# Weight blocks' low parts and sums by DMAs that add onto a negated copy; gated linear attention by chunks, each head over its own 64 rows

## Chip, cores and metric

One core of one Trainium2 chip. The metric is the device time of one execution, in microseconds; less is better. Before the change it is 478.68 us, the median of 3 runs (477.87 to 479.24).

## What is computed

One decoder layer over 1088 tokens (1024 of a prompt, and 64 that are 8 sequences of 8 new tokens), model width 1024, everything in float32. With `h = RMSNorm(x)` and one projection of `h`:

```
a, gl, zc, q, k, v, zg, lr = split(h @ w_in)          # 512,512,512,256,256,512,512,16 columns
u  = a * sigmoid(gl)
cv = swish(group_layer_norm(depthwise_causal_conv(u, width 31)))
cv = (cv @ w_pw + b_pw) * silu(zc)
gk = log_sigmoid(lr @ w_alpha + b_alpha) / 16          # forget gate
o, S = gla(q, k, v, gk, S0)                            # 4 heads, keys of 64, values of 128
o  = rms_norm_per_head(o) * silu(zg)
y  = final_rms_norm(x + concat[cv, o] @ w_out)
```

`gla` is linear attention by chunks of tokens: within a chunk `o = (mask(q_t k_t^T)) v + q_t S`, and between chunks `S = S * decay + k_dec^T v`. Besides `y` the last rows of `u` and the states `S` are returned.

## The kernel before

**Split operands.** A float32 product is made of three products in the faster float32r format: an operand is split into a high part (a copy rounded to float32r) and a low part (operand minus high part), and TensorE adds high by high, high by low and low by high in PSUM. `split` (L418) does it: ScalarE copies, VectorE subtracts. `load_split` (L515) loads a weight block of 128 x 512 values into a staging buffer (`wst`, 4 slots) and splits it into the pools `wh` and `wl` (8 slots each). A weight tile of 1024 x 128 is two such halves.

**Stages.** Tokens lie along the free axis in three chunks of 384, 384 and 320 (`CHUNKS`). In order of time: loading and RMSNorm; the projections `gl` and `a` (4 tiles each); `v` of the first two heads with the low-rank gate input; `q` and `k` of these heads with the linear attention between them; `v`, then `q` and `k` of the other two heads; `zc`; `zg` with the pointwise product; and the out projection. The convolution is 31 multiply-adds of 128 x 1024 values on VectorE for each of four channel tiles; `conv_tick` gives them a low priority, so that they fill what VectorE has free up to their normalization in the `zc` and `zg` stages.

**Linear attention.** `gla_tile(p, tk)` (L765) handles one pair of heads `p` and 128 tokens. The two heads lie in the 128 rows, 64 each. `q_chunk` keeps two copies of q, each with the other head's 64 rows set to zero (by GpSimd memsets), so that a product over all 128 rows yields one head alone. A tile has a transpose of k, two products `pa` (k by q), a masked copy on VectorE, two products `pS` into 64 rows each (in the tile `px`), two of the old state by q and two of values by masked scores (both into `po`), and the update of the state. All of them are float32, which TensorE runs as two passes each; the trace counts passes.

**Out projection.** Blocks of 512 x 512 are multiplied by a scheme of seven products of sums and differences (`pr1` to `pr7`). Sums of blocks of `w_out` are made in place on VectorE (`t1` to `t4`, L1198 to L1226) out of loaded blocks, and each operand is split as above (`parts`).

**Order.** Nothing is issued as written. Each helper adds an operation with a cost to a list, and `Program.schedule` plays the list on a model of the engines: an engine takes the ready operation of the highest priority (mostly the order of writing) whose buffers are free. The instruction streams of the engines are fixed in that order, and each then runs in order on the chip. Loads and stores are issued by SyncE; GpSimd does memsets alone.

Of the kernel before, what the change touches and what calls it, by code (L numbers as in the profile page):

```python
# [14 lines left out]
P = 128  # L15
# [116 lines left out]
class Program:  # L132
# [159 lines left out]
    def issue(self, preload, after):  # L292
        order = self.schedule()
        table = next(o.table for o in order if o.table is not None)
        preload(table)
        for o in order:
            if o.table is not None and o.table != table:
                table = o.table
                preload(table)
            i = o.fn().ins  # L300
            o.name = i.name
            for tl in o.allocs:
                if tl.before is not None:
                    for name in tl.before.seen.values():
                        after(i, name)
            for tl in o.tiles:
                tl.seen[(o.eng, i.name if o.eng == "SP" else "")] = i.name
# [3 lines left out]
def build(tc, A, O):  # L311
# [68 lines left out]
    def mm(ps, lhsT, rhs, start, stop, after=None):  # L380
# [3 lines left out]
        o = prog.add("PE", lambda: T.matmul(R(ps), R(lhsT), R(rhs), start=start, stop=stop, skip_group_check=True),  # L384
                     [ps], [lhsT, rhs], c, lag=lag)
        if after is not None:
            o.deps.add(after)
        return o
# [7 lines left out]
    with ctx:  # L396
# [31 lines left out]
        mask_p = cst[:, K_MP:K_MP + 2 * P].bitcast(U32)  # L428
# [9 lines left out]
        at_p = [VT(fixed, f"at{i}", [P, 2 * P], F32, f"at{i}") for i in range(2)]  # L438
# [89 lines left out]
        def wtile(kind, i):  # L528
            return [whalf(kind, i, h) for h in range(2)]
# [107 lines left out]
        def v_weights(p):  # L637
            cols = 272 if p == 0 else 256
            return cols, [load_split(f"v{p}{i}", A[f"wv{p}"][i], 2, cols) for i in range(4)]
# [102 lines left out]
        qx = {}  # L742
        o_t = [None] * 4

        def q_chunk(p, w, c):

            ep = gx[(p, c)][0]
            n = CHUNKS[c][1]
            other = un(f"qx{p}_{c}")
            ps = proj_chunk(f"q{p}", w, c)  # L750
            lo, hi = slice(0, 64), slice(64, P)
            prog.hold = True
            zero(other[lo, :n])
            stt(other[hi, :n], ps[hi], 0.125, ep[hi, :n], ALU.mult, ALU.mult)
            stt(ep[lo, :n], ps[lo], 0.125, ep[lo, :n], ALU.mult, ALU.mult)
            zero(ep[hi, :n])
            qx[(p, c)] = ep, other
# [7 lines left out]
        def gla_tile(p, tk):  # L765
            c = tk // 3
            off = tk * P - CHUNKS[c][0]
            s = slice(off, off + P)
            q, km = qx[(p, c)], gx[(p, c)][1][:, s]
            v = vslice(p, tk)  # L770
            if tk == 0:
                for j in range(2):
                    o_t[2 * p + j] = bt(f"o{2 * p + j}")
            hs = [slice(P * j, P * j + P) for j in range(2)]
            px = pt(f"px{p}_{tk}")
            pk, pS = px[:, 0:P], px[:, P:2 * P]
            transpose(pk, km, ident)
            kT = VT(sm, "kT", [P, P], F32, f"kT{p}_{tk}")
            act(kT, pk, AF.Copy)
            pa = pt(f"pa{p}_{tk}")  # L780
            for j in range(2):
                mm(pa[:, hs[j]], km, q[j][:, s], True, True)
            at = at_p[tk % 2]
            select(at, mask_p, pa[:, 0:2 * P])
            for j in range(2):
                r = slice(64 * j, 64 * j + 64)
                mm(pS[r], kT[:, r], v[:, hs[j]], True, True)

            po = pt(f"po{p}_{tk}")
            first = None  # L790
            if tk > 0:
                for j in range(2):
                    first = mm(po[:, hs[j]], St[p], q[j][:, s], first is None, False, first)
            for j in range(2):
                first = mm(po[:, hs[j]], v[:, hs[j]], at[:, hs[j]], first is None, True, first)
            Sn = VT(sm, "S", [P, P], F32, f"S{p}_{tk}")
            cf = g_c[p][:, tk + 1:tk + 2]
            if tk == 0:
                ts(Sn, pS, cf, None, ALU.mult, None)
            else:  # L800
                Sc = VT(sm, "S", [P, P], F32, f"Sc{p}_{tk}")
                act(Sc, St[p], AF.Copy, scale=cf)
                stt(Sn, pS, cf, Sc, ALU.mult, ALU.add)
            St[p] = Sn
            for j in range(2):
                act(o_t[2 * p + j][:, tk * P:(tk + 1) * P], po[:, hs[j]], AF.Copy)
            if tk == 7:
                dma(O["gla_p"][:, p], Sn)
# [7 lines left out]
        def gla_sample(p):  # L816
            s = slice(256, 320)
            q, km = qx[(p, 2)], gx[(p, 2)][1][:, s]
            v = v_s
            prog.step, prog.shift = STEP, 0  # L820
# [7 lines left out]
            for j in range(2):  # L828
                mm(pa[0:64, hs[j]], km, q[j][:, s], True, True)
            at = at_s  # L830
            select(at[0:64], mask_s, pa[0:64, 0:P])
            q2 = un(f"q2{p}")[:, 0:P]
            for j in range(2):
                act(q2[:, hs[j]], q[j][:, s], AF.Copy)
# [3 lines left out]
            for j in range(2):  # L838
                first = mm(po[:, hs[j]], v[:, j * P:(j + 1) * P], at[:, hs[j]], j == 0, False, first)
            for b in range(NB):  # L840
                bs = slice(b * LB, (b + 1) * LB)
                mm(po.split(64)[:, :, bs], S0[:, b, :], q2[:, :, bs], False, True, first)
# [154 lines left out]
        for p in range(2):  # L997
            wq, wk = wtile("q", p), wtile("k", p)
            s0_load(p)
            for c in range(3):  # L1000
                if (p, c) not in gx:
                    gates(p, c)
                q_chunk(p, wq, c)
                conv_tick(2)
                if c > 0:
                    gla_tile(p, 3 * c - 3)
                k_chunk(p, wk, c)
                conv_tick(2)
                if c > 0:
                    gla_tile(p, 3 * c - 2)  # L1010
                    gla_tile(p, 3 * c - 1)
            if p == 0:
                wv = v_weights(1)
                for tk in range(NTT):
                    v_tile(1, wv, tk)
                    conv_tick(2)
                    if tk < 2:
                        gla_tile(0, 6 + tk)
# [8 lines left out]
            else:  # L1027
                for i in range(4):
                    w = wtile("zc", i)
                    for c in range(3):  # L1030
                        zc_chunk(i, w, c)
                        conv_tick(5)
                        if i == 0:
                            if c < 2:
                                gla_tile(1, 6 + c)
# [39 lines left out]
        for i in range(4):  # L1075
            w = wtile("zg", i)
            if i == CN_LAST:
# [4 lines left out]
                wpw += [load_split(f"pw{j}", A["w_pw"][j], 4, P) for j in range(4)]  # L1082
# [12 lines left out]
        def b_load(name, e0, h, i):  # L1095
            st = VT(wst, "wst", [P, 512], F32, f"s_{name}{i}")
            dma(st, A["w_out"][e0 + i][:, 512 * h:512 * h + 512])
            return st

        def B11(n_, i):  # L1100
            return b_load(f"b11{n_}", 0, 0, i)

        def B12(n_, i):
            return b_load(f"b12{n_}", 0, 1, i)

        def B21(n_, i):
            return b_load(f"b21{n_}", 4, 0, i)

        def B22(n_, i):
            return b_load(f"b22{n_}", 4, 1, i)  # L1110
# [9 lines left out]
        def prep(name, a, b):  # L1120
            av, bv = [], []
            for i in range(4):
                av.append(parts(f"{name}a", i, a(i)))
                bv.append(parts(f"{name}b", i, b(i)))
# [11 lines left out]
        pr1 = prep("p1", lambda i: A11[i], lambda i: B11("p", i))  # L1136
# [70 lines left out]
        def t2(i):  # L1207
            tt(T_[i], B22("t", i), T_[i], ALU.subtract)
            return T_[i]
# [9 lines left out]
        def t3(i):  # L1219
            b = B22("u", i)  # L1220
            tt(b, b, B12("u", i), ALU.subtract)
            return b

        def t4(i):
            tt(T_[i], B21("u", i), T_[i], ALU.subtract)
            return T_[i]  # L1226
# [7 lines left out]
        pr2 = prep("p2", lambda i: A12[i], lambda i: B21("p", i))  # L1234
# [14 lines left out]
        pr3 = prep("p3", s4, lambda i: B22("p", i))  # L1249
# [11 lines left out]
        b12 = [parts("b12", i, B12("p", i)) for i in range(4)]  # L1261
# [110 lines left out]
```

## Time and profile before

| | us |
|---|---|
| median of 3 runs | 478.68 |
| the profiled execution | 479.08 |
| its span, from first to last instruction | 477.0 |
| TensorE busy | 465.4 |
| VectorE busy | 416.2 |
| ScalarE busy | 297.8 |
| GpSimd busy | 9.3 |

The profile is one execution. "PE" is TensorE's matmuls, "PEld" its weight loads, DVE VectorE, ACT ScalarE, POOL GpSimd, SP SyncE. Busy time of PE contains what its pipeline overlaps, so a pace is read from the starts of neighbours, not from the duration of one. Names as `px<-v,kT` are output and inputs by the program's tile names.

### The profile page before, as it was taken

How to read it: one execution, taken by the hardware profiler on the slowest of the kernel's cores; microseconds unless marked ns; L12 is line 12 of the kernel's file. 1: busy time of each engine (PE TensorE's matmuls, PEld its weight loads, DVE VectorE, ACT ScalarE, POOL GpSimd, SP SyncE). 2: the span in 40 equal slices, each digit the busy share in tenths (PEclk: the TensorE clock that was granted, in tenths of full speed). 3: DMA queues.
4: the chain of work that ended last, by engine and by line, in shares of the span. 5: the costliest groups of instructions: out<-in, count | busy, mean ns of one | idle time of the engine just before them, and what ended most of it. 6: DMA issues, size and time to landing. Idle time of an engine off the chain costs nothing.

```text
span 477.0 us, 7890 instructions
## 1 busy us (share of the span) xinstructions
PE 465.4 (98%) x2867; PEld 436.9 (92%) x2867; DVE 416.2 (87%) x669; ACT 297.8 (62%) x794; POOL 9.3 (2%) x33
## 2 busy tenths in 40 slices
PE   7999999999999999999999999999999999999983
PEld 6899999999999999999899999999999988788763
DVE  4999999999999999999998999983527579999896
ACT  6969569816660645694643696669637465666854
POOL 1000000000000000000000000000000000000000
PEclk9999999999999999999999999999999999999998
DMA  8910391212030110030010002010101364246765
GB/s 258 357 35 1 122 180 45 57 56 56 1 123 11 40 51 7 32 123 25 28 62 21 31 1 88 23 44 24 46 33 51 119 232 152 89 142 205 239 201 218
DMA packets 33238, 43.28 MB, mean 91 GB/s; under 512 B 11696, under 2 KB 16560, under 8 KB 33200
## 3 DMA queue, kind: packets, MB, share of 16 engines
q1 hardware_dynamic: 33200, 42.78, 27.9%
q8 instruction: 22, 0.36, 0.3%
q14 instruction: 16, 0.13, 0.1%
HBM read 36.58 MB, written 6.19 MB: 90 GB/s over the span
## 4 chain that ended last, share of the span: by engine, by line
PE 88%; DVE 4%; ACT 3%; DMA 2%; issue 1%; SPq 1%; DVEq 0%
PE pv L384 11%; PE p_zc L384 10%; PE p_zg L384 10%; PE ya L384 9%; PE p_gl L384 8%; PE p_a L384 8%; PE p_k L384 5%; PE p_q L384 5%; PE pw L384 5%; PE yc L384 4%; PE po L384 3%; PE pa L384 2%; DVE xr L343 1%; PE px L384 1%; DMA s_gl<-in_w_in 1%
## 5 line engine op out<-in xcount | busy, mean ns | idle before, releaser
L339 DVE SCALAR_TENSOR_TENSOR cv<-u,par,cv 128x1024 f32<-128x1024 f32 x120 | 150.5, 1274 | 0.2
L384 PE MATMUL pv<-h_v,hh 128*128 128x272 f32 (+1 forms) x128 | 37.2, 291 | 0.0
L384 PE MATMUL pv<-l_v,hh 128*128 128x272 f32 (+1 forms) x128 | 37.0, 289 | 0.0
L384 PE MATMUL pv<-h_v,hl 128*128 128x272 f32 (+1 forms) x128 | 37.0, 289 | 0.0
L384 PE MATMUL p_gl<-hh,h_gl 128*128 128x384 f32 (+1 forms) x96 | 32.4, 338 | 1.3 <-ACT hh L333 0.8
L333 ACT ACTIVATE pr<-us,par 128x64 f32<-128x64 f32 x124 | 32.2, 346 | 0.4 <-DMA us<-in_cc 0.4
L384 PE MATMUL p_zc<-hh,h_zc 128*128 128x384 f32 (+1 forms) x96 | 32.1, 335 | 0.0
L384 PE MATMUL p_zc<-hh,l_zc 128*128 128x384 f32 (+1 forms) x96 | 31.9, 332 | 0.0
L384 PE MATMUL p_zc<-hl,h_zc 128*128 128x384 f32 (+1 forms) x96 | 31.8, 331 | 0.0
L384 PE MATMUL p_gl<-hl,h_gl 128*128 128x384 f32 (+1 forms) x96 | 31.7, 330 | 0.1
L384 PE MATMUL p_gl<-hh,l_gl 128*128 128x384 f32 (+1 forms) x96 | 31.6, 329 | 0.2 <-DVE l_gl L343 0.2
L384 PE MATMUL p_a<-hh,l_a 128*128 128x384 f32 (+1 forms) x96 | 31.7, 331 | 0.0
L384 PE MATMUL p_zg<-hh,l_zg 128*128 128x384 f32 (+1 forms) x96 | 31.4, 328 | 0.0
L384 PE MATMUL p_a<-hh,h_a 128*128 128x384 f32 (+1 forms) x96 | 31.4, 327 | 0.0
L384 PE MATMUL p_a<-hl,h_a 128*128 128x384 f32 (+1 forms) x96 | 31.4, 327 | 0.0
L384 PE MATMUL p_zg<-hl,h_zg 128*128 128x384 f32 (+1 forms) x96 | 31.4, 327 | 0.0
L384 PE MATMUL p_zg<-hh,h_zg 128*128 128x384 f32 (+1 forms) x96 | 31.4, 327 | 0.0
L384 PEld LDWEIGHTS pv<-h_v,hh 128*128 128x128 f32 x128 | 24.1, 189 | 0.4 <-issue 0.3
L384 PEld LDWEIGHTS pv<-l_v,hh 128*128 128x128 f32 x128 | 24.1, 189 | 0.3 <-issue 0.3
L384 PEld LDWEIGHTS pv<-h_v,hl 128*128 128x128 f32 x128 | 24.1, 188 | 0.0
L384 PEld LDWEIGHTS p_gl<-hh,h_gl 128*128 128x128 f32 x96 | 18.0, 188 | 2.4 <-ACT hh L333 1.4
L384 PEld LDWEIGHTS p_gl<-hl,h_gl 128*128 128x128 f32 x96 | 18.0, 188 | 0.9 <-DVE hl L343 0.4
(341 smaller groups left out, 1344.6 us busy)
## 6 DMA issues: line engine op xcount, KB each, us to landing
xr<-in_x SPq DMA_DIRECT2D x16, 256.0 KB, 3.4
out_y<-xr SPq DMA_DIRECT2D x16, 256.0 KB, 2.5
x<-in_xT SPq DMA_DIRECT2D x16, 192.0 KB, 4.7
s_gl<-in_w_in SPq DMA_DIRECT2D x8, 256.0 KB, 4.7
s_a<-in_w_in SPq DMA_DIRECT2D x8, 256.0 KB, 4.2
s_zc<-in_w_in SPq DMA_DIRECT2D x8, 256.0 KB, 2.5
s_zg<-in_w_in SPq DMA_DIRECT2D x8, 256.0 KB, 2.6
x<-in_xT SPq DMA_DIRECT2D x8, 160.0 KB, 5.2
```

Source lines behind the costliest of these rows:

```text
L333: return S.activation(R(out), R(in_), func, **kw)
L339: prog.add("DVE", lambda: V.scalar_tensor_tensor(R(out), R(a), R(s), R(b), op0, op1), [out], [a, s, b], out.n / 0.96 + 67 + 62 * isinstanc ...
L343: prog.add("DVE", lambda: V.tensor_tensor(R(out), R(a), R(b), op), [out], [a, b], out.n / 0.96 + 67)
L384: o = prog.add("PE", lambda: T.matmul(R(ps), R(lhsT), R(rhs), start=start, stop=stop, skip_group_check=True), [ps], [lhsT, rhs], c, lag=lag)
```

## The change

It has two halves. First, for the weight blocks that are loaded after the first four tiles, the low part is no longer subtracted on VectorE: ScalarE writes the negated high part into the low part's buffer, and a DMA issued by GpSimd reads the block once more from memory and adds it onto that buffer (`low_part`, `load_parts`, `b_parts`). The sums of `w_out` blocks are made in the same way (`flip`). Second, the linear attention runs by chunks of three (or two) tiles in two functions, `gla_states` and `gla_out`. The products of k by q and of state by q run over the 64 rows of their own head, so q needs no zeros and no second copy; products that lie in different halves of the array are written one after another, and the planner books each of a pair at half the cost (`pair=True`).

```diff
+    def dma_add(out, in_):
+        prog.add("POOL", lambda: G.dma_start(R(out), R(in_), accum_op=ALU.add), [out], [in_], 1100,
+                 nbytes=out.n * 4 * P, lag=2400)
...
+        def low_part(hi, lo, src):
+            act(lo, hi.bitcast(F32), AF.Copy, scale=-1.0)
+            dma_add(lo, src)
+
+        def load_parts(name, src, k, m):
+            st = VT(wst, "wst", [P, k, m], F32, f"s_{name}")
+            hi = VT(wh, "wh", [P, k, m], F32R, f"h_{name}")
+            lo = VT(wl, "wl", [P, k, m], F32R, f"l_{name}")
+            dma(st, src)
+            act(hi, st, AF.Copy)
+            low_part(hi, lo, src)
+            return hi, lo
...
         def wtile(kind, i):
-            return [whalf(kind, i, h) for h in range(2)]
+            return [load_parts(f"{kind}{i}_{h}", A["w_in"][mt[(kind, i)]][:, 4 * h:4 * h + 4, :], 4, P)
+                    for h in range(2)]
...
         def q_chunk(p, w, c):
             ep = gx[(p, c)][0]
             n = CHUNKS[c][1]
-            other = un(f"qx{p}_{c}")
             ps = proj_chunk(f"q{p}", w, c)
-            ...
+            stt(ep[:, :n], ps, 0.125, ep[:, :n], ALU.mult, ALU.mult)
...
+        def gla_states(p, c):
+            nt = 3 if c < 2 else 2
+            m = nt * P
+            km = gx[(p, c)][1]
+            pk = pt(f"pk{p}_{c}")
+            for i in range(nt):
+                transpose(pk[:, P * i:P * i + P], km[:, P * i:P * i + P], ident)
+            kT = un(f"kT{p}_{c}")
+            act(kT[:, :m], pk[:, :m], AF.Copy)
+            pS = pt(f"px{p}_{c}")
+            for i in range(nt):
+                v = vslice(p, 3 * c + i)
+                for j in range(2):
+                    mm(pS[HR[j], P * i:P * i + P], kT[:, P * i + 64 * j:P * i + 64 * j + 64], v[:, P * j:P * j + P],
+                       True, True, pair=True)
+            gs[(p, c)] = before = []
+            for i in range(nt):
+                ...
+                    act(Sc, pS[:, P * i:P * i + P], AF.Copy, scale=cf)
+                    stt(Sn, St[p], cf, Sc, ALU.mult, ALU.add)
+                St[p] = Sn
...
+        def gla_out(p, c):
+            ...
+            pa = [pt(f"pa{p}_{c}_{j}") for j in range(2)]
+            po = [pt(f"po{p}_{c}_{j}") for j in range(2)]
+            last = gs[(p, c)][-1]
+            wait = [x[2] for x in last.tile.acc if x[1]]
+            for i in range(nt):
+                s = slice(P * i, P * i + P)
+                for j in range(2):
+                    mm(pa[j][:, s], km[HR[j], s], q[HR[j], s], True, True, wait, True)
+            first = [None] * 2
+            for i in range(nt):
+                s = slice(P * i, P * i + P)
+                S_ = gs[(p, c)][i]
+                if S_ is not None:
+                    for j in range(2):
+                        first[j] = mm(po[j][:, s], S_[HR[j]], q[HR[j], s], first[j] is None, False, [first[j]], True)
+            for j in range(2):
+                select(at_p[j][:, :m].split(P), mask_p.bcast([P, nt, P]), pa[j][:, :m].split(P))
+            for j in range(2):
+                for i in range(nt):
+                    s = slice(P * i, P * i + P)
+                    first[j] = mm(po[j][:, s], vslice(p, 3 * c + i)[:, P * j:P * j + P], at_p[j][:, s], False, True,
+                                  [first[j]])
+            for j in range(2):
+                if c == 0:
                     o_t[2 * p + j] = bt(f"o{2 * p + j}")
+                act(o_t[2 * p + j][:, t0:t0 + m], po[j][:, :m], AF.Copy)
...
+        def b_parts(name, i, e0, h):
+            st, src = VT(wst, "wst", [P, 512], F32, f"s_{name}{i}"), w_blk(e0 + i, h)
+            dma(st, src)
+            t_ = VT(big, "big", [P, 2, 512], F32R, f"{name}{i}")
+            act(t_[:, 0, :], st, AF.Copy)
+            low_part(t_[:, 0, :], t_[:, 1, :], src)
+            return t_
...
+        def flip(t_, src):
+            act(t_, t_, AF.Copy, scale=-1.0)
+            dma_add(t_, src)
+            return t_
+
         def t1(i):
             T_[i] = temp("T", i)
-            tt(T_[i], B12("t", i), B11("t", i), ALU.subtract)
-            return T_[i]
+            dma(T_[i], w_blk(i, 0))
+            return flip(T_[i], w_blk(i, 1))
...
         def t2(i):
-            tt(T_[i], B22("t", i), T_[i], ALU.subtract)
-            return T_[i]
+            return flip(T_[i], w_blk(4 + i, 1))
```

`t3` and `t4` change as `t1` and `t2` do, and `b_parts` stands for `parts` on the four plain blocks of `w_out` (`pr1`, `pr2`, `pr3` and `b12`). In `gla_sample`, which handles the 64 new tokens, the zeros move into a small tile of 128 columns.

## Rows read from the trace of the kernel before

**Rows 1.** Head of the page: span, and busy time (share) and instructions of each engine.

```profile
span 477.0 us, 7890 instructions
PE 465.4 (98%) x2867; PEld 436.9 (92%) x2867; DVE 416.2 (87%) x669; ACT 297.8 (62%) x794; POOL 9.3 (2%) x33
```

**Rows 2.** Windows: busy us (instructions) of each engine in three stretches.

```profile
core 0: us, PE busy (x) PEld busy (x) DVE busy (x) ACT busy (x) POOL busy (x), PEclk, DMA share, GB/s
0.00:307.50 307.50, 304.81 (x2022) 293.51 (x2023) 288.27 (x431) 193.10 (x573) 8.06 (x30) 1.00 0.24 70
28.20:429.00 400.80, 400.80 (x2534) 382.91 (x2535) 353.71 (x536) 243.59 (x666) 7.06 (x19) 1.00 0.21 63
381.20:456.20 75.00, 73.43 (x321) 58.81 (x320) 69.53 (x123) 50.51 (x111) 0.82 (x2) 1.00 0.53 182
```

**Rows 3.** Timeline of TensorE, end of the out projection: start, us, [idle before <- releaser].

```profile
443.42 11.19 PE L384 MATMUL ya<-p7b,p7a 128*128 128x512 f32 x48
456.17 2.10 PE L384 MATMUL ya<-p4b,p4a 128*128 128x512 f32 x8 [1.57 <-DVE xr L343]
```

**Rows 4.** Groups of TensorE by form, linear attention: busy us, mean ns of a pass.

```profile
L384 PE MATMUL pa<-ge,g 128*128 128x128 f32 x32 | 6.4, 281 | 0.0
L384 PE MATMUL po<-ge,S 128*128 128x128 f32 x28 | 5.6, 282 | 0.0
```

**Rows 5.** Timeline of TensorE around one tile of the linear attention.

```profile
148.83 0.39 PE L384 MATMUL pa<-ge,g 128*128 128x128 f32 x2
149.06 0.39 PE L384 MATMUL pa<-qx,g 128*128 128x128 f32 x2
149.20 0.42 PE L384 MATMUL p_k<-hh,h_k 128*128 128x384 f32 x1
149.46 0.34 PE L384 MATMUL p_k<-hl,h_k 128*128 128x384 f32 x1
149.73 0.44 PE L384 MATMUL px<-v,kT 128*64 128x128 f32 x4
150.10 0.44 PE L384 MATMUL p_k<-hh,l_k 128*128 128x384 f32 x1
150.38 0.34 PE L384 MATMUL p_k<-hh,h_k 128*128 128x384 f32 x1
150.56 0.34 PE L384 MATMUL p_k<-hl,h_k 128*128 128x384 f32 x1
```

**Rows 6.** Timeline of TensorE, last stretch: state products of the new tokens.

```profile
467.40 2.23 PE L384 MATMUL pSs<-vs,km 64*64 64x128 f32 x32
```

**Rows 7.** Groups of VectorE and ScalarE by form: busy us, mean ns of one.

```profile
L339 DVE SCALAR_TENSOR_TENSOR cv<-u,par,cv 128x1024 f32<-128x1024 f32 x120 | 150.5, 1274 | 0.2
L349 DVE TENSOR_SCALAR cv<-u,par 128x1024 f32<-128x1024 f32 x4 | 3.2, 804 | 0.0
L343 DVE TENSOR_TENSOR l_zg<-s_zg,h_zg 128x512 fp32r<-128x512 f32 x8 | 5.5, 687 | 7.1 <-ACT h_zg L333 7.1
L333 ACT ACTIVATE h_zg<-s_zg 128x512 fp32r<-128x512 f32 x8 | 5.1, 635 | 3.4 <-PE p_zg L384 1.8 <-PE p_zc L384 1.6
```

**Rows 8.** Chain that ended last: first use of gl's third tile; a store's issue.

```profile
60.65 11.90 PE p_gl L384 x72
...
442.10 0.35 SPq L377
```

**Rows 9.** Timeline of VectorE: low parts of that tile's two halves.

```profile
50.86 1.28 DVE L343 TENSOR_TENSOR l_gl<-s_gl,h_gl 128x512 fp32r<-128x512 f32 x2
```

**Rows 10.** DMA issues: count, KB each, median us from issue to landing.

```profile
s_zg<-in_w_in SPq DMA_DIRECT2D x8, 256.0 KB, 2.6
...
fg<-in_fg SPq DMA_DIRECT2D x1, 512.0 KB, 6.8
```

**Rows 11.** Instructions on tile p1b: count, duration ns min/median/max, first and last start.

```profile
L384 PE MATMUL ya<-p1b,p1a x48: 387/390/398, 381.0 to 391.8; 128*128 128x512 f32 x48
...
L343 DVE TENSOR_TENSOR p1b<-s_b11p,p1b x4: 680/681/691, 365.5 to 380.0; 128x512 fp32r<-128x512 f32 x4
```

More of the change, by code (lines that the diff above doesn't have):

```diff
@@ L378, in dma, with mm @@
                  nbytes=v.n * 4 * (v.part[1] - v.part[0]))
-    def mm(ps, lhsT, rhs, start, stop, after=None):
+    def dma_add(out, in_):
+        prog.add("POOL", lambda: G.dma_start(R(out), R(in_), accum_op=ALU.add), [out], [in_], 1100,
+                 nbytes=out.n * 4 * P, lag=2400)
+    def mm(ps, lhsT, rhs, start, stop, after=(), pair=False):
         n, m = rhs.n, lhsT.n
@@ L384, in mm @@
         o = prog.add("PE", lambda: T.matmul(R(ps), R(lhsT), R(rhs), start=start, stop=stop, skip_group_check=True),
-                     [ps], [lhsT, rhs], c, lag=lag)
-        if after is not None:
-            o.deps.add(after)
+                     [ps], [lhsT, rhs], c / 2 if pair else c, lag=lag)
+        o.deps.update(a for a in after if a is not None)
         return o
@@ L427, in build @@
         Jr, blkr, one_r = [VT(fixed, nm, [P, P], F32R, nm) for nm in ("Jr", "blkr", "one_r")]
-        mask_p = cst[:, K_MP:K_MP + 2 * P].bitcast(U32)
+        mask_p = cst[:, K_MP:K_MP + P].bitcast(U32).split(P)
         mask_s = cst[0:64, K_MS:K_MS + P].bitcast(U32)
@@ L437, in build @@
         eps = pc(C_EPS)
-        at_p = [VT(fixed, f"at{i}", [P, 2 * P], F32, f"at{i}") for i in range(2)]
+        at_p = [VT(fixed, f"at{i}", [P, 3 * P], F32, f"at{i}") for i in range(2)]
         at_s = VT(fixed, "ats", [P, P], F32, "ats")
@@ L638, in v_weights @@
             cols = 272 if p == 0 else 256
-            return cols, [load_split(f"v{p}{i}", A[f"wv{p}"][i], 2, cols) for i in range(4)]
+            return cols, [load_parts(f"v{p}{i}", A[f"wv{p}"][i], 2, cols) for i in range(4)]
         def v_tile(p, w, tk):
@@ L763, in k_chunk @@
             tt(em[:, :n], ps, em[:, :n], ALU.mult)
[L765 to L771, printed above, removed]
-                for j in range(2):
-                    o_t[2 * p + j] = bt(f"o{2 * p + j}")
[L774 to L808, printed above, removed]
@@ L817, in gla_sample @@
             s = slice(256, 320)
-            q, km = qx[(p, 2)], gx[(p, 2)][1][:, s]
+            q, km = [t_[:, s] for t_ in gx[(p, 2)]]
             v = v_s
+            q2 = un(f"q2{p}")[:, 0:P]
+            prog.hold = True
+            zero(q2)
+            for j in range(2):
+                act(q2[HR[j], 64 * j:64 * j + 64], q[HR[j]], AF.Copy)
             prog.step, prog.shift = STEP, 0
@@ L828, in gla_sample @@
             for j in range(2):
-                mm(pa[0:64, hs[j]], km, q[j][:, s], True, True)
+                mm(pa[0:64, hs[j]], km, q2[:, hs[j]], True, True)
             at = at_s
             select(at[0:64], mask_s, pa[0:64, 0:P])
-            q2 = un(f"q2{p}")[:, 0:P]
-            for j in range(2):
-                act(q2[:, hs[j]], q[j][:, s], AF.Copy)
             q2 = q2.split(64)
@@ L838, in gla_sample @@
             for j in range(2):
-                first = mm(po[:, hs[j]], v[:, j * P:(j + 1) * P], at[:, hs[j]], j == 0, False, first)
+                first = mm(po[:, hs[j]], v[:, j * P:(j + 1) * P], at[:, hs[j]], j == 0, False, [first])
             for b in range(NB):
                 bs = slice(b * LB, (b + 1) * LB)
-                mm(po.split(64)[:, :, bs], S0[:, b, :], q2[:, :, bs], False, True, first)
+                mm(po.split(64)[:, :, bs], S0[:, b, :], q2[:, :, bs], False, True, [first])
             for j in range(2):
@@ L1081, in build @@
                     act(zc[j], zc[j], AF.Silu)
-                wpw += [load_split(f"pw{j}", A["w_pw"][j], 4, P) for j in range(4)]
+                wpw += [load_parts(f"pw{j}", A["w_pw"][j], 4, P) for j in range(4)]
             for c in range(3):
@@ L1123, in prep @@
                 av.append(parts(f"{name}a", i, a(i)))
-                bv.append(parts(f"{name}b", i, b(i)))
+                bv.append(b_parts(f"{name}b", i, *b) if isinstance(b, tuple) else parts(f"{name}b", i, b(i)))
             return av, bv
@@ L1134, in product @@
                     mm(acc[t], av[k][:, 1, ts_], bv[k][:, 0, :], False, k == 3)
-        pr1 = prep("p1", lambda i: A11[i], lambda i: B11("p", i))
+        pr1 = prep("p1", lambda i: A11[i], (0, 0))
         fg = VT(big, "big", [P, DM], F32, "fg")
@@ L1260, in build @@
         psr = pt("pys1")
-        b12 = [parts("b12", i, B12("p", i)) for i in range(4)]
+        b12 = [b_parts("b12", i, 0, 1) for i in range(4)]
         samples_half(1, True, False, pr3[1], 4, psr)
```

66 lines of the change are left out of this document (32 added, 34 removed).

## Prediction, made before the changed kernel was run

> **What bounds the kernel now.** I read the page's head first, then the windows, the waits of TensorE in its timeline, and last the linear attention in the timeline, row by row. TensorE is busy 465.4 of 477.0 us, VectorE 416.2, ScalarE 297.8 [rows 1]. From 28.2 to 429 us TensorE has no idle time at all: 400.8 of 400.8 [rows 2]. The 11.6 us that it lacks lie at the start (loads and RMSNorm), in the tail after the last product, and in one wait of 1.57 us before the last product `p4` of the out projection, which VectorE ends [rows 3]. So the time is TensorE's list of work; an edit counts where it shortens that list or where it makes TensorE wait. VectorE is the second bound: up to 307.5 us it is busy 288.3 [rows 2], much of it with the convolution's taps [rows 7].
>
> **The linear attention.** The passes of one product start some 0.11 us apart: of two neighbouring products `pa`, two passes each, the first starts at 148.83 and the second at 149.06, 0.23 us later [rows 5]. The old kernel issues 16 tiles x 2 `pa` and 14 tiles x 2 products of state by q (both kinds also on the twin copy of q): twice the 32 and 28 passes of the rows, 120 passes [rows 4], x 0.112 (0.23 / 2, less rounding) = 13.4 us.
>
> Written per head over 64 rows, two neighbours use different halves of the array. The trace has no such pair. Its nearest row is `pSs`, whose neighbours write different 64 columns of the array: 32 passes, the last starting (2.23 - 0.27 for its own length) = 1.96 us after the first, 0.063 a pass [rows 6]. Bounds: 0.112 if row halves don't overlap, 0.056 if they overlap fully. I take 0.063, by the row that is nearest: 120 x 0.063 = 7.6.
>
> Entering and leaving such a form costs something. Products of `q` or `k` at 384 columns start 0.18 apart (150.38 to 150.56); into the four passes of `px` it is 0.27 (149.46 to 149.73), out of them 0.28 (150.10 to 150.38) [rows 5]: 0.09 + 0.10 = 0.19 for an excursion. The new kernel makes the `pa` and the state products in one burst for each chunk, 6 bursts: 1.1 us. Saved: 13.4 - 7.6 - 1.1 = 4.7 us (full overlap 5.6; no overlap a loss of 1.1).
>
> The Trainium skill, TensorEngine Tiling (Array Packing), Key Properties, says that a change of tiling mode drains the engine. That speaks against the change, which puts more products into such a mode; the 0.19 us an excursion agrees with it. Its figure of up to 2x for a contraction of 64 rows would give 6.7 us for the 120 passes.
>
> The state products `pS` now make 16 excursions of four passes: 0.37 (149.73 to 150.10) + 0.19 = 0.56 each [rows 5], 9.0 us. Afterwards the same 64 passes stand in 6 groups: 64 x 0.063 + 6 x 0.19 = 5.2. Saved 3.8. Transposes and the products with values stay as many; but any float32 group between projections lengthens the next start (0.26 at 149.20 against 0.18, so 0.08 [rows 5]). At most 16 x 3 such insertions become 6 x 4, so 0 to 1.9 us; I take 0.8, since many groups stand side by side already. Together the list shortens by 4.7 + 3.8 + 0.8 = 9.3 us.
>
> Cost on the same path: a chunk now runs transposes, copy, `pS`, three state updates in a row, then `pa`, two selects of up to 384 columns, and `po`, and TensorE needs projections to fill the gaps. All of `k`, the next `q`, `v` or `zc` lies there as cover. A chunk also holds up to 6 of 8 PSUM banks. Bounds: nothing if cover suffices; 4 us a chunk, 24 us, if TensorE sat through the whole chain (a copy and three updates of some 0.8 with their handovers, two selects). I take 1 us in all, near the lower end, because the old tiles have the same kind of chain and show no idle time in the rows [rows 2].
>
> **VectorE.** A low part is 0.687 us [rows 7]. 44 go from the projections and pointwise weights, 16 from `w_out`, and 16 subtractions for sums: 76 x 0.69 = 52 us of 416. Nearly all before 307.5 us is hidden, since TensorE never waits there [rows 2]; but it is needed. If TensorE's list there gets 9.3 us shorter, VectorE would have 307.5 - 288.3 - 9.3 = 10 us of room; about 40 of the low parts lie there and give back 27. So VectorE isn't what is late next. In the out projection it is busy 69.5 of 75.0 [rows 2] and loses 28 operations, 19 us. The wait of 1.57 us before `p4` [rows 3] I count as gone: the sums for it no longer need VectorE or a staging buffer. Gain 1.6 (bounds 0 and 1.6).
>
> **ScalarE** gets 76 copies at 0.635 [rows 7], 48 us, and loses some 4 in wider copies of the attention: 342 in all. In the out projection it has 50.5 of 75.0 [rows 2], and 28 copies more make 68.3. That is tight, and it replaces VectorE as the fuller engine there; I count nothing, because a sum can be flipped as soon as its old value is split, ten and more us ahead.
>
> **The adding DMAs.** No DMA of the trace adds, and none is issued by GpSimd. Issue: SyncE's takes 0.35 [rows 8], the lower bound; the upper is that GpSimd is held until the block has landed, 2.6 or more [rows 10]. I take about 1, nearer to the row of an issue. Landing: from 2.6 (256 KB, a plain load) to 6.8 (the 512 KB load, since an add reads two operands of 256 KB) [rows 10]; I take 5. A low part then comes 0.64 + 1 + 5 - 0.69 = 6 us later than now (bounds 2.9 to 9.4). Is there room? The tightest weight half of the projections is `gl`'s third tile: low parts done at 52.14 [rows 9], used from 60.65 [rows 8], 8.5 us. That holds at 6, and lacks 0.9 at the worst; the second half is used 2 us later still. `b_parts` of `pr1` are tighter: its last low part starts at 380.0 and the product at 381.0 [rows 11]. But only the last two blocks of four wait; planned with this delay, the first two blocks of all four output tiles come first, 4 x 7 products at about 0.23 (11.19 / 48 [rows 3]), 6.4 us of cover. Nothing counted, worst case 4.
>
> SBUF — State Buffer, of the Trainium skill, warns (SBUF: two separate sides) that GpSimd can't write descriptors while VectorE runs an operation in a mode that takes both ports, a rule against issuing these DMAs from GpSimd. The trace's sign of that mode is a tap of 804 ns where the ordinary ones take 1274 [rows 7]: four such operations and a few short ones at the end, so by the rule a delay of at most 0.8 us a time, inside the room above.
>
> **Sum.** The profiled execution is 479.08, 2.08 over its span and 0.4 over the median of 478.68, less than a measurement here can tell (about 0.3%, 1.4 us). 479.08 - 9.3 - 1.6 + 1.0 = **469.2 us**, 2% less. Own range of this case: 479.08 - (5.6 + 3.8 + 1.9 + 1.6) = 466 to 474, the upper end with 4 us more of waits and the lower bounds of the small terms.
>
> **Rivals.**
>
> *Row halves don't overlap.* The passes keep 0.112: instead of 4.7 saved, 1.1 lost, 475.0 us (473 to 477). For it: no row shows two products on different rows. Against: `px` and `pSs` do overlap on different columns [rows 5, 6]. Chance 0.14.
>
> *The chunks starve TensorE.* The chain of a chunk is half uncovered, 2 us x 6 more than counted, because PSUM banks held by the attention leave the projections too few: 469.2 + 10 = 479, no change; wholly uncovered 492. For it: 6 of 8 banks, where a tile held 3. Against: idle time of zero with the old chain. Chance 0.12, a quarter of it at over 481.
>
> *GpSimd is the bound of the out projection* (the other side: slower). It issues in order, waits for each negated copy (0.64) and is held until the add has landed: 0.35 + 0.64 + 2.6 = 3.6 us an add. 32 adds lie between the first use of `p1b`'s buffers (about 364) and the last split for `p4` (about 452), 88 us. 32 x 3.6 = 115, 27 us late: 496 us. It decides from (88 + 10) / 32 = 3.1 us an add; under 2.75 it costs nothing. For it: GpSimd has issued no DMA here. Against: SyncE isn't held by its own loads. Chance 0.10.
>
> **Numbers.** Forecast 0.62, first rival 0.14, second 0.12, third 0.10; 0.02 left over. Faster by over 0.3%: 0.62 + 0.14 and a little of the second, 0.77. Within 0.3%: 0.07, the middle of the second. Slower: 0.16. The range takes the forecast's own, the first rival and the second up to its middle: 463 to 480, the lower end 3 us under the case's bound for a plan that merges more groups than I count; the third rival is left out.
>
> **What would show it.** Right: `pa` and state products in bursts with passes about 0.06 us apart; `px` in six groups; TensorE without idle time from 28 to the out projection, and its list some 9 us shorter; no wait before `p4`; low parts landing several us before their first product; VectorE near 360 us busy. Wrong: passes of a burst at 0.11 (first rival); idle time of TensorE before `pa` or `po`, released by a state or a select, or by a PSUM copy (second); idle time before products with `l_` tiles or `p1b`, `p3b`, `p4b`, released by a DMA of GpSimd, and GpSimd issues over 3 us apart (third). The prediction is wrong if TensorE's idle time grows by more than its list shrinks, 9 us.

## The result, and the profile after

The changed kernel takes **491.14 us** (median of 4 runs, 489.66 to 492.34) against 478.27 (477.31 to 479.24) of the kernel before beside it: a ratio of 1.0262 [1.0235, 1.0288] (in brackets, here and below, the 95% interval). It is 2.6% slower, where 2% faster was forecast. The profiled execution took 491.32 us.

The head of the page after, the slices (40 equal parts of the span, in tenths), and the DMA queues (packets, MB, share of 16 engines' span):

```profile
span 489.6 us, 7973 instructions
PE 466.6 (95%) x2867; PEld 435.5 (89%) x2867; DVE 369.1 (75%) x583; ACT 334.3 (68%) x840; POOL 71.2 (15%) x99
...
PEclk9999999997999999999999999999999899989997
DMA  8900897553036350044524044433018985987865
...
q1 hardware_dynamic: 30896, 38.59, 25.6%
q0 software_dynamic: 10944, 19.99, 24.5%
```

VectorE lost 47 us [rows 1], of the 52 that it was to lose. TensorE's idle time grew from 11.6 to 23.0 us, and its busy time from 465.4 to 466.6 although its list is shorter. The new line is `q0`, the 76 adds: they hold 24.5% of all sixteen DMA engines, almost as much as `q1`, which moves twice the bytes. So an add of 256 KB takes 0.245 x 489.6 / 76 = **1.58 us of all sixteen engines**. A plain transfer of the same size takes 0.82 by SyncE's queue of before (27.9% of 477.0 us for 42.78 MB):

```profile
q1 hardware_dynamic: 33200, 42.78, 27.9%
```

The share adds up the times of packets, so in a full stretch it can pass 1 (1.05 in `late_adds`, below).

The windows after, with TensorE's granted clock, the DMA share and GB/s as the last three columns, and two of them before:

```profile
core 0: us, PE busy (x) PEld busy (x) DVE busy (x) ACT busy (x) POOL busy (x), PEclk, DMA share, GB/s
...
60.60:108.40 47.80, 47.80 (x293) 47.80 (x292) 39.76 (x37) 35.28 (x120) 7.34 (x10) 1.00 0.71 142
108.40:135.70 27.30, 22.63 (x165) 22.44 (x164) 25.19 (x39) 14.74 (x56) 0.86 (x1) 0.87 0.23 46
...
381.20:410.00 28.80, 25.73 (x107) 20.41 (x106) 17.77 (x29) 20.02 (x40) 7.85 (x10) 0.94 0.86 190
410.00:440.00 30.00, 26.17 (x104) 20.81 (x103) 17.54 (x29) 22.50 (x42) 12.16 (x14) 0.89 0.83 167
440.00:470.00 30.00, 28.61 (x125) 22.63 (x124) 21.77 (x44) 23.87 (x59) 4.65 (x7) 1.00 0.77 207
```

```profile
381.20:410.00 28.80, 28.80 (x127) 23.17 (x127) 26.01 (x45) 18.80 (x37) 0.41 (x1) 1.00 0.47 164
410.00:440.00 30.00, 30.00 (x133) 24.36 (x132) 28.51 (x49) 19.25 (x38) 0.00 (x0) 1.00 0.46 161
```

Between 410 and 440 us the engines are 0.83 busy and move 167 GB/s. Before, the same window had 0.46 and 161: the same bytes a second for nearly twice the occupancy. VectorE is idle two fifths of the windows from 381 to 440, and TensorE, which had no idle time there, has 3.1 and 3.8 us and runs below its full clock.

TensorE's waits after (us in total, times, longest):

```profile
PE lrtp L398 <- issue: 4.7, 1, 4.7
PE yc L389 <- ACT p5b L333: 3.8, 1, 3.8
PE ya L389 <- DMA p1b<-in_w_out: 3.1, 1, 3.1
...
PE ya L389 <- DVE xr L343: 0.7, 1, 0.7
```

Three stretches make up the difference of the spans. From the end of the values' products `pv` on the first tile to `p_zg`, where the linear attention lies, the time falls from 172.0 to 165.9 us (-6.1). The `pv` stage before it goes from 27.1 to 34.0 (+6.9), with the wait at `lrtp`. The out projection to the end goes from 96.0 to 108.2 (+12.2), with the waits at `p1b` and `p5b`. Together +13.0; the rest, -0.4, lies outside them.

**The wait at `lrtp`** begins 54 us earlier, with four loads for the convolution's cache. The issues of SyncE, before and after, and the DMA issues after (count, KB each, median us to landing):

```profile
58.22 3.08 SPq L377 DMA_DIRECT2D us<-in_cc  x4
...
59.01 9.73 SPq L377 DMA_DIRECT2D us<-in_cc  x4
```

```profile
l_zg<-in_w_in POOLq DMA_DIRECT2D x8, 256.0 KB, 4.0
...
l_gl<-in_w_in POOLq DMA_DIRECT2D x4, 256.0 KB, 7.4
...
p1b<-in_w_out POOLq DMA_DIRECT2D x4, 256.0 KB, 7.5
...
s_p3b<-in_w_out SPq DMA_DIRECT2D x4, 256.0 KB, 11.2
...
us<-in_cc SPq DMA_DIRECT2D x4, 120.0 KB, 9.0
```

Eight adds for `gl` and `a` are issued from 48.6 to 61.9 us and take 7.3 to 7.4 us each to landing; the cache's loads, 3.9 us to landing before, take 9.0 among them, and their issues spread over 9.7 us instead of 3.1. ScalarE waits 7.5 us for `us`, VectorE 7.1 for ScalarE's products `pr`, and VectorE is then 5 us behind until it owes TensorE `lrst` at 113: it writes it at 117.6 where it did at 112.6, and `lrtp`, for whose wait the profile names no releaser, starts at 117.9. After the wait the products run at half the clock for a while, as their starts show:

```profile
119.78 0.43 PE L389 MATMUL pv<-h_v,hh 128*128 128x272 f32 x1
120.00 0.43 PE L389 MATMUL pv<-l_v,hh 128*128 128x272 f32 x1
...
123.35 0.29 PE L389 MATMUL pv<-h_v,hh 128*128 128x272 f32 x1
123.48 0.29 PE L389 MATMUL pv<-l_v,hh 128*128 128x272 f32 x1
```

0.225 us a product up to 122.3, and 0.126 behind it: the level of 1.2 GHz and then that of 2.4. So a wait of 4.7 us cost 6.9. The same follows the waits at `p1b` and `p5b` (granted clock 0.94 and 0.89 in their windows).

**Linear attention.** One chunk in the timeline of TensorE (start, length):

```profile
156.33 0.88 PE L389 MATMUL px<-v,kT 128*64 128x128 f32 x12
157.13 0.44 PE L389 MATMUL p_k<-hh,h_k 128*128 128x384 f32 x1
...
160.48 0.94 PE L389 MATMUL pa<-ge,g 64*128 64x128 f32 x12
161.25 0.61 PE L389 MATMUL po<-ge,S 64*128 64x128 f32 x8
161.79 0.41 PE L389 MATMUL pg<-lrT,was 128*128 128x320 f32 x1
```

Twelve `pa` passes over 64 rows take 161.25 - 160.48 = 0.77 us to the next group, 0.064 a pass with the entry into the group, where the old ones took some 0.11 [rows 5]: row halves overlap.

### The profile page after: what moved, and what is told of

The parts are those of the page before. It is cut to its first block, busy times and chain, and to the rows that moved or that the text cites. A ratio compares the mean times of both kernels' runs of the same rounds, so it can differ in the third digit from the quotient of the medians.

```text
span 489.6 us, 7973 instructions
## 1 busy us (share of the span) xinstructions
PE 466.6 (95%) x2867; PEld 435.5 (89%) x2867; DVE 369.1 (75%) x583; ACT 334.3 (68%) x840; POOL 71.2 (15%) x99
## 3 DMA queue, kind: packets, MB, share of 16 engines
q0 software_dynamic: 10944, 19.99, 24.5%
## 4 chain that ended last, share of the span: by engine, by line
PE 69%; DMA 9%; issue 9%; ACT 6%; DVE 3%; POOL 2%; SPq 1%; POOLq 0%; DVEq 0%; ACTq 0%
PE pv L389 11%; PE p_zc L389 10%; PE p_gl L389 8%; PE p_a L389 8%; PE p_zg L389 8%; PE p_k L389 5%; PE p_q L389 5%; PE pw L389 4%; PE po L389 2%; DMA T<-in_w_out 2%; ACT sq L333 2%; DMA U<-in_w_out 2%; DMA out_y<-xr 1%; DMA s_b<-in_w_out 1%; DMA s_gl<-in_w_in 1%
## 5 line engine op out<-in xcount | busy, mean ns | idle before, releaser
L389 PE MATMUL pv<-h_v,hh 128*128 128x272 f32 (+1 forms) x128 | 38.4, 300 | 0.0
L389 PEld LDWEIGHTS pv<-h_v,hl 128*128 128x128 f32 x128 | 25.1, 196 | 0.2 <-issue 0.2
L343 DVE TENSOR_TENSOR o<-o,zg 128x384 f32<-128x384 f32 (+1 forms) x12 | 6.3, 535 | 23.3 <-ACT zg L333 23.3
```

The lines of the kernel that those rows point to most:

```text
L343: prog.add("DVE", lambda: V.tensor_tensor(R(out), R(a), R(b), op), [out], [a, b], out.n / 0.96 + 67)
```

## Experiments

The kernel before took 478.8 to 479.1 us beside all of them. Each result is the median time in us and its ratio to the kernel before. "Parts by VectorE" means a staged block and a subtraction, as before the change.

**1. The two halves of the change.** `gla_only` has the attention by chunks, with all 76 low parts and sums by VectorE; `adds_only` has the adds and the old attention.

```diff
 def load_parts(name, src, k, m):       # gla_only; w_out's parts and sums likewise
...
-    act(hi, st, AF.Copy)
-    low_part(hi, lo, src)
-    return hi, lo
+    return load_split(name, src, k, m)
```

> Only the linear attention by chunks; every low part and sum on VectorE as before. Theory (the attention shortens TensorE's list, the adding DMAs lose it again by crowding the 16 DMA engines): in the changed kernel the stretch from q of the first heads to the end of zc took 165.9 us against 171.9, so this run is 6 us under before, 472 (470 to 474). Rival (chunks starve TensorE once VectorE still has its low parts): 478 or more, with idle time of TensorE between 135 and 310 us.

> Only the adding DMAs; the linear attention tile by tile as before. Theory: the changed kernel's time plus the 6 us that the attention saves, 497 (493 to 500). Rival (the loss comes from the attention's chunks or from the two together): 485 or less.

Measured: `gla_only` 474.44 us, 0.9903 [0.9883, 0.9924], 0.4 above its range; `adds_only` 499.07, 1.0402 [1.0372, 1.0432]. The attention alone is a gain of 4.6 us, the adds alone a loss of 20. TensorE's busy time in `gla_only` is 459.6 us, 5.8 under before; the full change has 7.0 more, the same list at the lower clock.

**2. Adds in one stage only**, with the attention by chunks: `adds_proj` keeps those of the projections and pointwise weights (44), `adds_out` those of the out projection (32).

> Attention by chunks, adding DMAs for the projections' and pointwise weights alone; the out projection on VectorE as before. Theory: 472 plus the wait near 113 us (4.7) and the halved clock behind it (2): 479 (476 to 481). Rival (only the out projection loses): 472, no wait of TensorE near 113 us.

> Attention by chunks, adding DMAs in the out projection alone; low parts of projections on VectorE as before. Theory: 472 plus the 12 us by which the changed kernel's out projection is longer, 484 (481 to 487). Rival (the early wait made the late part late): 475 or less.

Measured: 479.64, 1.0022 [0.9995, 1.0049], and 487.84, 1.0187 [1.0143, 1.0230], the second 0.8 above its range. Over `gla_only` that is 5.2 and 13.4; together 18.6, and the full change stands 16.7 over it. `adds_proj` has the wait of 4.9 us at `lrtp` and no other of its kind; `adds_out` has those at `p5b` (4.3) and `p1b` (3.6), and not the first.

**3. A plain copy instead of the add**, from the same queue; the additions are left out.

```diff
-        prog.add("POOL", lambda: G.dma_start(R(out), R(in_), accum_op=ALU.add), [out], [in_], 1100,
+        prog.add("POOL", lambda: G.dma_start(R(out), R(in_)), [out], [in_], 1100,
...
```

> All 76 adding DMAs of the changed kernel are plain copies from HBM instead, of the same 256 KB from the same blocks to the same tiles, on GpSimd's queue, at the same places in every order (the low parts and sums are then left out of the arithmetic). Theory (the adding itself fills the DMA engines: 1.58 us of all sixteen for an add of 256 KB, against about 0.82 for a plain load): the copies' queue falls from 24.5% to about 13% of the span, the DMA share between 410 and 440 from 0.83 to about 0.6, the three waits of TensorE of 3 to 5 us shrink, and the time is 478 (473 to 484). Rival 1 (the order is what costs: rounding, negating, then a transfer from GpSimd's queue, one after the other, whatever the transfer does): 491 (488 to 493), with the three waits as they are. Rival 2 (only the extra bytes count): 491 too, but with the DMA share above 0.8 and the queue's share unchanged.

Measured: 477.48 us, 0.9951 [0.9930, 0.9972]. Its queue on the page, and its out projection in the windows:

```profile
q0 software_dynamic: 9920, 19.99, 15.2%
```

```profile
410.00:440.00 30.00, 29.63 (x129) 23.86 (x129) 20.35 (x33) 27.46 (x53) 9.32 (x18) 1.00 0.71 220
```

The same 19.99 MB in the same order take 0.152 x 478.3 / 76 = 0.96 us of the engines each instead of 1.58, and 13.7 of the 16.7 us are gone. So neither the bytes nor the order rounding, negating, transfer is what costs most: it is the addition in the DMA engines. The 3.0 us that stay over `gla_only` go with smaller waits, 2.8 us at `p1b` and 1.8 at `lrtp`.

**4. A plan that knows of late landings:** the planner is told 6.0 us instead of 2.4.

> The planner is told that an add lands 6.0 us after its issue rather than 2.4, and puts the readers and the issues elsewhere; the same 76 adds. Theory (the DMA engines are full in the out projection, .83 to .86 of them for 60 us): a better order moves waits about and gains little: 488 (485 to 493). Rival (the plan, which reckons with landings half as long as they are, is what makes products wait): the waits of 3 to 5 us go and the time is 478 (475 to 482).

Measured: 491.57, 1.0252 [1.0225, 1.0279], no change. The wait at `p1b` goes; one of 5.0 us before `pSs` comes, and those at `lrtp` (4.7) and `p5b` (4.3) stay.

**5. No adds around the cache's loads**, in the changed kernel and in one without adds in the out projection.

```diff
-wg, wa_ = wtile("gl", ct), wtile("a", ct)
+wg, wa_ = [[whalf(k_, ct, h) for h in range(2)] for k_ in ("gl", "a")]
```

> The first low parts of the gl and a weights that the change makes by adds (tiles 2 and 3 of each) are made by VectorE, so that no add is under way while the cache of the convolution is loaded, before 61 us; all else as in the changed kernel. Theory (these adds delay the four loads us<-in_cc from 3.9 to 9.0 us, ScalarE and VectorE pass it on, and TensorE waits 4.7 us at 113 and then runs 6.8 us at the lower clock): the wait is gone and the time is 484.5 (483 to 486). Rival (the wait comes of the order that attention by chunks gives VectorE and ScalarE there, and the adds have no part in it): 491 (489 to 493).

> Attention by chunks; the out projection's parts and sums and the first gl and a tiles by VectorE; adds only for the low parts of the other projections and of the pointwise weights, where the DMA share is 0.1 to 0.4 without them. Theory (an add costs nothing where the DMA engines have room, and takes work from VectorE that stands just ahead of the normalization's sums): the wait of 4.9 us of the kernel with all projection adds is gone, the waits for ScalarE's squares of 2.3 us that the kernel without adds has at 310 to 380 stay away too, and the time is 472 (470.5 to 474), faster than the 474.4 of attention by chunks alone. Rival 1 (adds cost a little wherever they are, 5 us over 44 of them): 477 to 479. Rival 2 (neither cost nor gain): 474.4 (473.8 to 475).

Measured: `cache_clear` 486.87, 1.0149 [1.0106, 1.0191], a little over the theory's range; the wait at `lrtp` is gone, and the stretch to 135.7 has a clock of 1.00 again. `quiet_adds` 473.52, 0.9868 [0.9845, 0.9891]: with 36 adds left, where the DMA engines have room, the adds cost nothing that shows. Against `gla_only` it can't be told apart (the intervals overlap), so the gain that its theory hoped for isn't shown. Its queue of adds:

```profile
q0 software_dynamic: 5184, 9.51, 12.7%
```

That is 0.127 x 471.8 / 36 = 1.66 us of the sixteen engines an add, no less than in the changed kernel: the crowding in its out projection doesn't explain the 1.58.

**6. Which adds of the out projection.** On the base of `quiet_adds`: only the 16 low parts, or only the 16 sums, by adds.

> The quiet adds of the 473.5 us kernel, and in the out projection the 16 low parts of weight blocks by adds as well, its 16 sums and differences of blocks by VectorE. Theory (what costs is the occupancy of the DMA engines): 16 adds of 1.58 us bring 25 us of all sixteen engines and save no load, so the DMA share between 381 and 440 goes from about 0.5 to about 0.75, p1b comes late, and the time is 480 (477 to 483), about two thirds of the 13.4 us that all 32 adds cost. Rival (each product pays for its own chain of rounding, negating and adding, with room on the engines or without): p1b's wait of 3 us with its clock, 477 to 478.5, and nothing at p5b.

> The quiet adds of the 473.5 us kernel, and in the out projection the 16 sums and differences of weight blocks by adds as well, its 16 low parts by VectorE. Theory (occupancy): 16 adds bring 25 us of the engines and save 16 plain loads of 0.82 us, 13 us, so the DMA share between 381 and 440 rises by 0.15 only and the time is 476.5 (474 to 479). Rival (each product pays for its chain: load, negate, add, then round): p5b's wait of 4 us with the lower clock behind it, 479 to 481.

Measured: `out_lows` 487.19, 1.0178 [1.0146, 1.0211]; `out_sums` 473.35, 0.9885 [0.9851, 0.9918]. Against `quiet_adds` the low parts cost 13.7 us, all that the 32 adds cost, and the sums nothing on balance (a wait of 2.1 us before `p6` comes, that of 1.8 before `p4` goes). TensorE's waits in `out_lows`:

```profile
PE pys L389 <- DMA b<-in_w_out: 4.4, 3, 3.6
PE pSs L389 <- DVE km L361: 3.7, 1, 3.7
PE ya L389 <- DMA p1b<-in_w_out: 3.6, 2, 3.2
```

Both theories missed, and the mean share can't tell the two kernels apart: from 381.2 to 440 us it is 0.65 in `out_lows` and 0.62 in `out_sums` (0.50 in `quiet_adds`). They differ in where the engines are full and in how soon a result is read, so four more kernels take these apart.

**7. Occupancy without a reader.** 16 adds of 192 KB onto tiles that nothing reads, started where the low parts' adds would be (`unread_by_act`), and the same kernel without them (`no_unread`), on the base of `quiet_adds`.

```diff
 split(t_[:, 0, :], t_[:, 1, :], st)
+z_ = VT(unit, "unit", [P, 384], F32, f"z_{name}{i}")
+act(z_, t_[:, 0, 0:384].bitcast(F32), AF.Copy)
+dma_add(z_, src[:, 0:384])              # not in no_unread
```

> The 473.5 us kernel with 16 adds of 192 KB onto tiles that nothing reads, one for each block of weights rounded in the out projection; ScalarE copies the rounded block (128 by 384) into the tile first, so that each add starts where the low part's add would. Theory 1 (fullness): 19 us of the engines in 60, the share goes from 0.5 to about 0.75, the loads of the blocks come late, and against the same kernel without these adds the time rises by 4 to 8 us: 478 to 482. Theory 2 (exposed landings): nobody waits for these adds; loads come later by 1 to 3 us but have that room: 474.5 (473.5 to 476).

> The same 16 copies by ScalarE, without the adds behind them: 16 times about 0.4 us on an engine that is busy 65% there. Both theories: 474 (473 to 475.5). If it is above that, ScalarE's copies cost, and the unread adds' cost is read as the difference of the two kernels.

Measured: 487.12, 1.0143 [1.0097, 1.0189], and 476.23, 0.9934 [0.9906, 0.9963]: **10.9 us from 16 adds for which no product waits**, more than the 4 to 8 of theory 1. `no_unread` lies 0.7 above its range and 2.7 over `quiet_adds`, so ScalarE's copies cost too, and the adds are read against it. Waits of TensorE, windows, and what SyncE's queue waited for from 376 to 392 us, in `unread_by_act`:

```profile
PE ya L389 <- DVE xr L343: 9.2, 1, 9.2
PE yc L389 <- ACT p5b L333: 4.8, 1, 4.8
```

```profile
381.20:395.00 13.80, 13.80 (x63) 11.17 (x62) 6.47 (x12) 6.59 (x13) 1.65 (x2) 1.00 0.84 228
395.00:410.00 15.00, 10.62 (x47) 8.22 (x45) 15.00 (x26) 10.29 (x22) 0.86 (x1) 0.95 0.29 100
```

```profile
SPq L377 <- DMA s_b12t<-in_w_out: 5.8, 1, 5.8
```

The first plain load `s_b11t`, issued at 379.05 us, takes 9.4 us to landing where it takes 3.6 without the unread adds (the four `s_b12t` have medians of 6.3 and 3.5). VectorE waits 7.3 us for it and has 6.5 us of work in 13.8. SyncE's queue stands 5.8 us for an `s_b12t` and 2.4 for VectorE's sum `T`, and issues the next `s_b11t` at 389.27 instead of 382.39. TensorE runs dry at 405.6, in the middle of `p5`, and before `p4` it waits for VectorE 5.1 us longer than in `no_unread`. In that stretch SyncE's loads and VectorE's work stand in the same order in both kernels. The same window and waits of `no_unread`:

```profile
381.20:395.00 13.80, 13.80 (x62) 11.21 (x61) 12.98 (x22) 8.21 (x17) 0.00 (x0) 1.00 0.49 165
```

```profile
PE ya L389 <- DVE xr L343: 4.1, 1, 4.1
```

**8. An exposed landing with little occupancy, and most adds without it.** `first_lows`: only the four low parts `p1b` by adds, on `quiet_adds`. `late_adds`: all but those of `p1b` and `b12`, 24 of 32.

> The 473.5 us kernel with the four low parts p1b of the first product of the out projection by adds, nothing else. Theory 1 (fullness of the DMA engines): four adds are 6.3 us of the engines, and the time is 473.5 to 475. Theory 2 (an add's landing stands between the rounding and the product that reads it, and here nothing covers it): TensorE waits some 3 us for p1b at 381, loses some more to the lower clock behind it, and the time is 478 (476.5 to 479.5), from four adds as much as a third of what all 32 cost.

> The 473.5 us kernel with 24 of the out projection's 32 adds: all sums, and the low parts p2b and p3b; those of the first product (p1b) and of the last block (b12) by VectorE. Theory 1 (fullness): 24 adds leave the DMA share between 381 and 440 near 0.75, and the time is 480 to 484. Theory 2 (exposed landings): the two places without cover are gone, p5b's sums remain, and the time is 475.5 (473 to 478).

Measured: `first_lows` 476.70, 0.9949 [0.9925, 0.9973], 3.2 over its base; TensorE waits 3.0 and 1.2 us for `p1b`, as theory 2 said. `late_adds` 478.03, 0.9983 [0.9962, 1.0004], 4.5 over it and at the upper end of theory 2's range. Its wait and its window of that time:

```profile
PE yc L389 <- ACT p5b L333: 5.4, 1, 5.4
```

```profile
410.00:425.00 15.00, 9.64 (x33) 7.45 (x32) 6.25 (x10) 10.16 (x19) 6.99 (x8) 0.77 1.05 216
```

The engines are full (1.05) where adds for `p3b` and for the sums fall together, and `p5b` waits for its sum's DMA. So both causes are there: four adds just ahead of their product cost 3.2 us, and 24 others cost 4.5, with a wait at a sum in a full stretch where `out_sums` (share 0.82 there) has none.

**9. Unread transfers anchored by GpSimd copies** instead of ScalarE's (24 of 192 KB, adds or plain loads):

> The 473.5 us kernel with 24 adds of 192 KB more in the out projection, onto tiles of their own that nothing reads (GpSimd copies 128 by 384 elements into each first, so that each starts when its block of weights has been rounded); no product waits for them. Theory (the occupancy delays the loads that others need): 24 times 1.19 us is 28.5 us of the engines, the DMA share between 381 and 440 goes from 0.5 to about 0.8, VectorE gets its blocks late, and the time is 478 (475 to 484). Rival (only products that wait for an add pay): 473.5 (472.5 to 475).

> As the kernel with unread adds, but the 24 transfers are plain loads of the same 192 KB onto the same tiles, from the same queue. Theory (occupancy, of which a plain load takes some 0.6 to 0.7 us where an add takes 1.19): DMA share about 0.68, 475 (473.5 to 477), about a third of what the unread adds cost. Rival (the bytes or GpSimd's copies cost, whatever the transfer does): the same time as with unread adds.

Measured: 490.72, 1.0249 [1.0201, 1.0297], and 485.58, 1.0151 [1.0116, 1.0186], both far above the theory and no match for the rivals. They don't price the transfers alone: GpSimd's copies, in the timeline of `unread_loads`, ran beside VectorE for up to 3.1 us each,

```profile
407.65 3.10 POOL L1147 COPY z_p6b<-p6b 128x384 f32<-128x384 f32 x1
...
421.49 0.60 POOL L1147 COPY z_p3b<-p3b 128x384 f32<-128x384 f32 x1 [0.20 <-ACT p3b L333]
```

and VectorE got through 20 instructions between 410 and 425 us where it did 25 in `quiet_adds`, busy in both: its operations on 128 by 512 values took up to 1.02 us there beside a copy, and 0.67 to 0.69 in `quiet_adds`. The Trainium skill, SBUF — State Buffer, Who interferes with whom, says that a VectorE instruction with two inputs in SBUF contends with a GpSimd instruction that reads SBUF; the trace agrees. The difference of the two kernels, 5.1 us, is again the price of adding. What GpSimd's copies cost by themselves no run shows.

## Why the prediction was wrong

**The step that failed** is "The adding DMAs ... Nothing counted". It priced an add by its issue and by its landing, each as if alone, and asked whether its own reader had room. It put at nothing what an add takes from the other transfers; the runs show 1.58 us of all sixteen engines for each, 120 us of the span for the 76. The loads beside it land late, and work that never touches an add waits. Experiment 3 shows the cause by taking the addition away (13.7 of 16.7 us back), experiment 7 by adds that nobody reads (10.9 us), experiment 5 for the wait at `lrtp`.

**Issue**: about 1 us was taken; GpSimd's groups after (busy us, mean ns of one) show 0.86 to 0.96:

```profile
L382 POOL DMA_DIRECT2D T<-in_w_out x12 | 10.4, 865 | 24.4 <-ACT T L333 13.2 <-PE pys L389 5.3 <-ACT ms L333 4.7
```

**Landing**: 5 was taken, from 2.6 to 6.8. The medians are 4.0 (`l_zg`) to 8.6 (`p2b`); the upper bound fell where the engines are fullest. The Trainium skill, DMA: Bandwidth & Descriptors, Anatomy of one DMA, gives for a DMA issued by GpSimd 2.0 us and bytes over 436 GB/s, an estimate of 2.6 for 256 KB. The trace has 2.6 for plain loads, but by SyncE [rows 10]; GpSimd's plain copies in `copy_not_add` took 3.0 and more (median of `l_pw`), its adds 4.0 and more (`l_zg`).

**Room.** For `gl`'s third tile it held: no product waits for an `l_` tile. For `p1b` it didn't: 6.4 us of cover were counted, and the wait begins after 14 products, 3.4 us in, since the plan reckoned with a landing of 2.4 us. The "worst case 4" was the case (3.1 and the clock behind it); `first_lows` prices it at 3.2 us by itself.

**The clock** had no term. Each of the three waits (4.7, 3.1 and 3.8 us) is followed by products at 1.2 GHz. At `lrtp` that makes 6.9 out of 4.7; the products ran at the lower level for 4.4 us there, not 6.8 as the expectation of `cache_clear` has it. In all TensorE's busy time is 7.0 us over `gla_only`.

**Attention.** Passes and bursts were right: `pa` and the products of state by q were put at 13.4 us before and 8.7 after, 4.7 saved; summed in the timeline from each group's start to the next, they are 13.5, 8.9 and 4.7. Of the 3.8 for `px` the half that lay in its passes came (6.3 to 4.4 us). The half for entering and leaving, and the 0.8 for fewer groups, didn't: it had to show as shorter projection products around the groups, and those of q, k, v and zc in that stretch take 124.1 us in `gla_only`, where they took 123.3. Not counted were the transposes, 0.8 us shorter side by side (2.0 to 1.3). In all 7.0 us are saved in that stretch of `gla_only`, and 6.1 in the full change, of the 9.3.

**Rivals.** Row halves do overlap, so the first is false. No `pa` or `po` waits, so the second is false. The third had the sign, but by another mechanism, so its 496 is near by luck: GpSimd isn't held (0.86 us an add, far under 3.1), and the bound that it should have named is the sixteen DMA engines. The wait before `p4` didn't vanish; it is 0.75 us of 1.57.

**What stays open** is how the 13.4 us of the out projection divide: `first_lows`, `late_adds` and `unread_by_act` overlap in what they change, and each alters the order of the rest. That the 16 sums cost nothing and the 16 low parts 13.7 goes with stretches in which the share is 0.97 and 0.87 (`out_lows`, 381 to 395 and 440 to 455), and with `p1b` and `b12`, which are read at once; no run separates these two further.

## What to carry to other kernels

When work moves from a compute engine to DMAs, cost it as occupancy of the sixteen engines beside the transfers that are there, not as a latency of its own: here a share of 0.46 became 0.83 at the same GB/s. Read the share in short pieces, since a mean over 59 us of 0.62 and of 0.65 stood for nothing lost and for 13.7 us. Look for the victims among loads that have nothing to do with the change, and follow the queue behind each. VectorE was the second bound on the page, but it had only one wait of TensorE's to give back, 1.57 us before `p4` [rows 3]; relieving it bought nothing that shows: `quiet_adds` and `out_sums` (473.5 and 473.4 us) can't be told from the kernel without any adds (474.4), all some 1% under the kernel before.

## What the runs showed of the hardware

- An add from HBM onto SBUF holds the sixteen engines 1.58 us for 256 KB (1.66 in `quiet_adds`), a plain transfer from the same queue 0.96 (`copy_not_add`), SyncE's plain transfers 0.82 (before).
- Products over 64 rows of the array overlap almost fully with a neighbour on the other half: 0.064 us a pass with the entry, against some 0.11.
- GpSimd's copies of 128 by 384 beside VectorE took from 0.5 to 3.1 us, VectorE's operations of 128 by 512 beside them up to 1.02 instead of 0.68 (`unread_loads`).
- The waits of TensorE of 3.1, 3.8 and 4.7 us in the changed kernel were each followed by products at the lower clock level, for 4.4 us after the wait at `lrtp`.
